# A decoder layer in split float32 on one core: the ten seven-product pairs of the last product at every second place instead of partly two in a row

## The chip, the core and the metric

The kernel runs on one core of a Trainium2 chip. The core has a matrix engine (TensorE, PE in the profile; its weight loads are listed apart as PEld), a vector engine (DVE), a scalar engine (ACT), a GpSimd engine (POOL) and a queue that issues transfers (SP). The engines run their own instruction lists in order and wait for each other through semaphores; transfers between main memory and the on-chip memory run beside them. The metric is the time of one execution on the device in microseconds (us).

## What is computed

One decoder layer for 256 tokens of width 2048, in float32. A first half (attention, a gated matrix memory, gates, an output projection) is left as it is by the change. The second half is a gated feed-forward block with a short convolution:

```python
h2 = rmsnorm(x, norm2_g[l])
u = causal_dwconv(jnp.einsum('bsd,df->bsf', h2, w_up[l]), conv_w[l], conv_b[l])
u_gate, u_val = u[..., :D_FF], u[..., D_FF:]
x = x + jnp.einsum('bsf,fd->bsd', jax.nn.silu(u_gate) * u_val, w_down[l])
```

`D_FF` is 5632. The last line holds the last product, which the change is about: 256 x 5632 by 5632 x 2048, added to x.

## The kernel before

**Split operands.** Every float32 operand is split in two: a high part that the matrix engine's fast float32 form takes exactly (`wh` for a weight), and the rest (`wl`). A product is three matmuls: high weight with both parts of the activation, low weight with its high part. Splitting weights is work for two engines. For each piece of a weight chunk ACT copies it into `wh` (line 169) and DVE subtracts to get `wl` (line 170). `wh` and `wl` have three buffers each, so piece n can only be split when PE has finished piece n - 3.

**Chunks and pairs.** Weights arrive in chunks of 1 MB (`raw`, three buffers, SP queue, line 132). In the last product one chunk is a pair: two steps of 128 along the 5632, by 1024 columns. There are 22 pairs for each of two column blocks, called y0 and y1 after their tiles. The accumulators of a block are `y0q` and `y0p` (or `y1q`, `y1p`).

**Two kinds of pair.** A plain pair ("p") is two pieces of 1024 columns and eight products of 128 x 512, 24 matmuls. A seven-product pair ("S") does the same block by a Strassen-like scheme with seven products, 21 matmuls. It has four pieces: "b" (1024 columns, straight from `raw`), "b21" (512 columns, straight from `raw`), "t13" (1024, sums) and "t24" (1024, sums). The sums of weights are formed by DVE in one tile `sums`: line 154 (1024 columns, the t13 half), line 161 and line 164 (512 each, the t24 half). The sums of activations were formed once in the stage before and stored in main memory (`se`, `s_dram`, lines 934 to 940); line 952 brings them back on POOL's queue, one load of 768 KB (`s_ops`) for two S pairs. Three such tiles fit at first; the next load waits until the tile of two S pairs ago has been read for the last time, and in y1 the tiles of finished activations come free as well. After the last S pair of a block the four sums of products are added into the result (line 298) while the remaining plain pairs run, then the plain accumulators (line 974), and the result goes out.

**What sets the order.** `Y_PAIRS` (line 39) gives the kind of each of the 22 pairs, for both blocks. `next_sub(3)` (line 175) splits three pieces ahead. A scheduler then orders each engine's list and may move an instruction ahead of others: it puts line 154 for the next S pair, which needs only the next chunk, early, between the two sums pieces of the S pair now in work. All lines 154 stand behind the last step of the up stage on DVE (the split of the last activations, `ghl`, line 196; the order is asked for in line 153). The stage before (up) computes `ghl`; its last matmuls, evacuation and split overlap the first pair of y0.

Chunks are numbered through the program: `raw204` is pair 0 of y0, `raw226` pair 0 of y1; pieces are numbered too, `wl434` being the first of y0.

Of the kernel before, what the change touches and what calls it, by code (L numbers as in the profile page):

```python
# [35 lines left out]
PLAIN = "p" * 8  # L36
G_PAIRS = "pSpSpSpp"
WO_PAIRS = "pSpSpppp"
Y_PAIRS = "ppp" + "SSpSp" * 3 + "Sp" + "pp"
N_S = Y_PAIRS.count("S")  # L40


# [18 lines left out]
def trunk(ctx: ExitStack, tc: tile.TileContext, a):  # L61
# [44 lines left out]
    def add_pairs(ap, patterns):  # L106
        for i, kind in enumerate("".join(patterns)):
            pieces = ("b", "b21", "t13", "t24") if kind == "S" else ("whole", "whole")
            add_chunk(ap[i], 2048, pieces)
# [8 lines left out]
    subs_of[n + 1], subs_of[n + 2] = subs_of[n + 2], subs_of[n + 1]  # L118
    add_pairs(a["w_dn"], [Y_PAIRS] * 2)

# [800 lines left out]
    for j in range(NF):  # L921
# [11 lines left out]
        m = j // 2  # L933
        if Y_PAIRS[m] == "S":
            se = big.tile([P, 2, 3 * P], F32R, tag="mv", name=f"se{m}")
# [7 lines left out]

    s_pos = [m for m, kind in enumerate(Y_PAIRS) if kind == "S"]
    ring = []
# [8 lines left out]
    def sums_of(b, m):  # L954
        g, (r, i) = g_pairs[m], divmod(s_pos.index(m) + b * N_S, 2)
        if i == 0:
            load_sums()
        at = [ring[r][:, q * P : (q + 1) * P] for q in range(6 * i, 6 * i + 6)]
        return [(g[:, 0, 0, P:], g[:, 0, 1, P:])] + [(at[c], at[3 + c]) for c in range(3)]
# [3 lines left out]
    for b in range(2):  # L963
# [5 lines left out]
        y_ops = Lazy(lambda m, b=b: sums_of(b, m))  # L969
        q = s_block(f"y{b}", g_pairs, y_ops, Y_PAIRS, pools, dst)  # L970
        for h in range(2):
# [80 lines left out]
```

## Time and profile before

| what | us |
|---|---|
| median of three runs (lowest, highest) | 1402.92 (1402.15, 1404.12) |
| the profiled execution's own time | 1393.67 |
| its span | 1391.9 |
| block y0, first matmul to first of y1 | 1150.7 to 1269.7 |
| block y1, first matmul to last | 1269.7 to 1387.2 |

The profiled execution is some 9 us shorter than the median of the runs shown, and differences are taken against its own time. The page's first part gives busy time by engine over the whole span: PE 99 %, DVE 77 %, ACT 55 %. A busy PE includes matmuls whose modelled ends overlap the next start, so small stalls must be read from starts in the timeline, where rows give start, duration, engine, line, operation, tiles and count, and in brackets the idle time before and what ended it.

### The profile page before, as it was taken

How to read it: one execution, taken by the hardware profiler on the slowest of the kernel's cores; microseconds unless marked ns; L12 is line 12 of the kernel's file. 1: busy time of each engine (PE TensorE's matmuls, PEld its weight loads, DVE VectorE, ACT ScalarE, POOL GpSimd, SP SyncE). 2: the span in 40 equal slices, each digit the busy share in tenths (PEclk: the TensorE clock that was granted, in tenths of full speed). 3: DMA queues.
4: the chain of work that ended last, by engine and by line, in shares of the span. 5: the costliest groups of instructions: out<-in, count | busy, mean ns of one | idle time of the engine just before them, and what ended most of it. 6: DMA issues, size and time to landing. Idle time of an engine off the chain costs nothing.

```text
span 1391.9 us, 18433 instructions
## 1 busy us (share of the span) xinstructions
PE 1375.6 (99%) x6940; PEld 1157.2 (83%) x6940; DVE 1070.9 (77%) x1524; ACT 767.2 (55%) x1096; POOL 40.4 (3%) x73
## 2 busy tenths in 40 slices
PE   9999999999999999999999999999999999999998
PEld 8878888887888888888888888888888887778776
DVE  5655766556888867777878888888878888887987
ACT  6645554444665544555655555555655655553553
POOL 2101000000000000000000000000000000000000
PEclk9999999999999999999999999999999999999999
DMA  8645454443554565555555655655555657668553
GB/s 312 229 165 184 179 209 155 152 151 134 196 215 182 214 241 194 190 220 203 191 186 194 218 193 190 222 186 196 201 212 194 230 196 266 226 251 291 205 209 119
DMA packets 44073, 281.76 MB, mean 202 GB/s; under 512 B 5008, under 2 KB 5024, under 8 KB 13264
## 3 DMA queue, kind: packets, MB, share of 16 engines
q1 hardware_dynamic: 39168, 260.20, 52.4%
q0 software_dynamic: 4672, 20.38, 4.2%
q8 instruction: 54, 0.88, 0.2%
q14 instruction: 35, 0.29, 0.1%
q10 hardware_dynamic: 144, 0.02, 0.0%
HBM read 272.45 MB, written 8.13 MB: 202 GB/s over the span
## 4 chain that ended last, share of the span: by engine, by line
PE 96%; DVE 1%; issue 1%; ACT 1%; DMA 1%; POOL 0%; DVEq 0%; ACTq 0%; POOLq 0%
PE up L230 35%; PE p L230 6%; PE y1q L230 6%; PE y0q L230 5%; PE mog L230 3%; PE fq L230 3%; PE mv L230 3%; PE fk L230 3%; PE fv L230 3%; PE wo0q L230 3%; PE wo1q L230 3%; PE g1q L230 2%; PE g3q L230 2%; PE g2q L230 2%; PE g0q L230 2%; PE y1p L230 2%
## 5 line engine op out<-in xcount | busy, mean ns | idle before, releaser
L169 ACT ACTIVATE wh<-raw 128x1024 fp32r<-128x1024 f32 (+2 forms) x496 | 502.7, 1017 | 473.9 <-PE up L230 117.9
L170 DVE TENSOR_TENSOR wl<-raw,wh 128x1024 fp32r<-128x1024 f32 (+2 forms) x496 | 575.1, 1169 | 205.3 <-ACT wh L169 203.5
L230 PE MATMUL up<-h,wh 128*128 128x512 f32 x1408 | 488.6, 394 | 0.0
L230 PE MATMUL up<-h,wl 128*128 128x256 f32 x1408 | 390.0, 277 | 0.0
L230 PEld LDWEIGHTS up<-h,wh 128*128 128x128 f32 x1408 | 263.9, 188 | 61.4 <-DVE h L199 0.2
L230 PEld LDWEIGHTS up<-h,wl 128*128 128x128 f32 x1408 | 264.4, 188 | 0.1
L170 DVE TENSOR_TENSOR wl<-sums,wh 128x1024 fp32r<-128x1024 f32 x66 | 80.6, 1222 | 43.9 <-ACT wh L169 43.5
L169 ACT ACTIVATE wh<-sums 128x1024 fp32r<-128x1024 f32 x66 | 69.9, 1060 | 78.6 <-PE y0q L230 16.6
L909 DVE SCALAR_TENSOR_TENSOR t<-u,cst,t 128x256 f32<-128x256 f32 x176 | 84.7, 481 | 3.8 <-ACT t L907 0.7
L230 PE MATMUL p<-wh,am 128*128 128x512 f32 x256 | 79.6, 392 | 0.0
L230 PE MATMUL y1q<-wh,ghl 128*128 128x512 f32 x232 | 71.7, 390 | 0.0
L230 PE MATMUL y0q<-wh,ghl 128*128 128x512 f32 x232 | 71.7, 390 | 0.0
L230 PEld LDWEIGHTS p<-wh,am 128*128 128x128 f32 x256 | 47.6, 188 | 9.7
L907 ACT ACTIVATE t<-u,cst 128x256 f32<-128x256 f32 x88 | 52.0, 591 | 2.4 <-DVE u L904 1.9
L230 PEld LDWEIGHTS y1q<-wh,ghl 128*128 128x128 f32 x232 | 43.6, 188 | 9.2
L230 PEld LDWEIGHTS y0q<-wh,ghl 128*128 128x128 f32 x232 | 43.5, 188 | 9.1
L230 PE MATMUL p<-wl,am 128*128 128x512 f32 x128 | 49.9, 390 | 0.0
L230 PE MATMUL y1q<-wl,ghl 128*128 128x512 f32 x116 | 44.8, 391 | 0.0
L230 PE MATMUL y0q<-wl,ghl 128*128 128x512 f32 x116 | 44.8, 390 | 0.0
L154 DVE TENSOR_TENSOR sums<-raw 128x1024 f32<-128x1024 f32 x33 | 40.4, 1223 | 4.7 <-DMA raw<-in_w_dn 3.0
L230 PE MATMUL mog<-wh,hT 128*128 128x348 f32 (+1 forms) x192 | 42.4, 331 | 1.3 <-ACT wh L169 1.3
L230 PE MATMUL g0q<-wh,hN 128*128 128x512 f32 x128 | 41.3, 401 | 0.0
(370 smaller groups left out, 2064.0 us busy)
## 6 DMA issues: line engine op xcount, KB each, us to landing
raw<-in_w_up SPq DMA_DIRECT2D x88, 1024.0 KB, 4.9
raw<-in_w_dn SPq DMA_DIRECT2D x44, 1024.0 KB, 4.9
raw<-in_w_g SPq DMA_DIRECT2D x32, 1024.0 KB, 4.9
raw<-in_w_fox SPq DMA_DIRECT2D x24, 1024.0 KB, 4.9
raw<-in_w_p SPq DMA_DIRECT2D x16, 1024.0 KB, 4.8
raw<-in_w_out SPq DMA_DIRECT2D x16, 1024.0 KB, 4.8
raw<-in_w_mqk SPq DMA_DIRECT2D x8, 1024.0 KB, 4.8
raw<-in_w_mv SPq DMA_DIRECT2D x8, 1024.0 KB, 4.8
```

Source lines behind the costliest of these rows:

```text
L154: nc.vector.tensor_tensor(sums[:, :1024].rearrange("p (i c) -> p i c", i=2), raw[:, :512].unsqueeze(1).to_broadcast([P, 2, 512]), src.rear ...
L169: nc.scalar.activation(wh[:, :n], src, AF.Copy)
L170: nc.vector.tensor_tensor(wl[:, :n], src, wh[:, :n].bitcast(F32), ALU.subtract)
L230: nc.tensor.matmul(out, lhsT, rhs, start=start, stop=stop)
L907: nc.scalar.activation(t, u[:, 2:], AF.Identity, scale=w[2], bias=w[3])
L909: nc.vector.scalar_tensor_tensor(out=t, in0=u[:, i : i + S], scalar=w[i], in1=t, op0=ALU.mult, op1=ALU.add)
```

## The change

One line. `Y_PAIRS` was `pppSSpSpSSpSpSSpSpSppp` (S pairs at places 3, 4, 6, 8, 9, 11, 13, 14, 16 and 18) and becomes `pSpSpSpSpSpSpSpSpSpSpp` (places 1, 3, 5 and so on to 19). There are ten S and twelve p in both, so the number of matmuls, splits, sums and bytes is the same.

```diff
-Y_PAIRS = "ppp" + "SSpSp" * 3 + "Sp" + "pp"
+Y_PAIRS = "p" + "Sp" * 10 + "p"
```

The scheduler's order changes with it. At the end of the up stage, DVE's list before, from the last activations (`gv`, `ghl`) to the first sums; the first S pair is `raw207`, and `raw206` is still a plain pair:

```order
L170 TENSOR_TENSOR wl437_10360<-raw205_10274,wh437_10359 128x1024
L909 SCALAR_TENSOR_TENSOR t_10320<-u0_5502,cst_75,t_10320 128x256 x2
L930 TENSOR_TENSOR gv_10218<-sg_10271,t_10320 128x256
L170 TENSOR_TENSOR wl438_10378<-raw206_10337,wh438_10377 128x1024
L196 TENSOR_TENSOR ghl10_5500<-gv_10218,ghl10_5500 128x2x256
L154 TENSOR_TENSOR sums207_10411<-raw207_10375 128x1024
L170 TENSOR_TENSOR wl439_10394<-raw206_10337,wh439_10393 128x1024
L161 TENSOR_TENSOR sums207_10411<-raw207_10375,sums207_10411 128x512
```

The same place of the changed kernel's list, where the first S pair is `raw205` and `wl437` is its piece b21:

```order
L170 TENSOR_TENSOR wl437_10363<-raw205_10274,wh437_10362 128x512
L909 SCALAR_TENSOR_TENSOR t_10320<-u0_5502,cst_75,t_10320 128x256 x2
L930 TENSOR_TENSOR gv_10218<-sg_10271,t_10320 128x256
L196 TENSOR_TENSOR ghl10_5500<-gv_10218,ghl10_5500 128x2x256
L154 TENSOR_TENSOR sums205_10343<-raw205_10274 128x1024
L161 TENSOR_TENSOR sums205_10343<-raw205_10274,sums205_10343 128x512
L164 TENSOR_TENSOR sums205_10343<-raw205_10274,sums205_10343 128x512
L170 TENSOR_TENSOR wl438_10384<-sums205_10343,wh438_10383 128x1024
L170 TENSOR_TENSOR wl439_10398<-sums205_10343,wh439_10397 128x1024
```

The first sums still stand behind the last activations, but now they belong to the second pair of y0, not to the fourth; `wl438` and `wl439` are its pieces t13 and t24.

Further on, DVE's list before where two S pairs follow each other (`raw207`, `raw208`), from the split of the first one's t13 to that of the second one's t24:

```order
L170 TENSOR_TENSOR wl442_10452<-sums207_10411,wh442_10451 128x1024
L154 TENSOR_TENSOR sums207_10411<-raw208_10409 128x1024
L170 TENSOR_TENSOR wl443_10466<-sums207_10411,wh443_10465 128x1024
L170 TENSOR_TENSOR wl444_10474<-raw208_10409,wh444_10473 128x1024
L161 TENSOR_TENSOR sums207_10411<-raw208_10409,sums207_10411 128x512
L170 TENSOR_TENSOR wl445_10485<-raw208_10409,wh445_10484 128x512
L164 TENSOR_TENSOR sums207_10411<-raw208_10409,sums207_10411 128x512
L170 TENSOR_TENSOR wl446_10498<-sums207_10411,wh446_10497 128x1024
L170 TENSOR_TENSOR wl447_10508<-sums207_10411,wh447_10507 128x1024
```

The changed kernel's list over one period, from the S pair `raw209` over the plain pair `raw210` to the S pair `raw211`:

```order
L170 TENSOR_TENSOR wl450_10542<-sums205_10343,wh450_10541 128x1024
L154 TENSOR_TENSOR sums205_10343<-raw211_10538 128x1024
L170 TENSOR_TENSOR wl451_10552<-sums205_10343,wh451_10551 128x1024
L170 TENSOR_TENSOR wl452_10559<-raw210_10500,wh452_10558 128x1024
L170 TENSOR_TENSOR wl453_10569<-raw210_10500,wh453_10568 128x1024
L170 TENSOR_TENSOR wl454_10582<-raw211_10538,wh454_10581 128x1024
L161 TENSOR_TENSOR sums205_10343<-raw211_10538,sums205_10343 128x512
L170 TENSOR_TENSOR wl455_10599<-raw211_10538,wh455_10598 128x512
L164 TENSOR_TENSOR sums205_10343<-raw211_10538,sums205_10343 128x512
L170 TENSOR_TENSOR wl456_10618<-sums205_10343,wh456_10617 128x1024
```

Two plain pieces (`wl452`, `wl453`) now always stand between the pieces of two S pairs, and line 154 for the next S pair always stands ahead of the split of the current one's t24 (`wl451`). Before, that was so at the same relation of pairs only where a p stood between.

## The prediction

> **What bounds the kernel now.** I first read the busy time of the two blocks of the last product (windows view: us, then busy us of PE, PEld, DVE, ACT, POOL, then granted clock, DMA share, GB/s).
>
> ```profile
> 1150.70:1269.70 119.00, 115.14 (x500) 91.76 (x499) 101.80 (x112) 63.46 (x69) 3.19 (x6) 1.00 0.68 246
> 1269.70:1387.20 117.50, 115.08 (x499) 91.54 (x498) 99.38 (x105) 60.38 (x64) 1.79 (x3) 1.00 0.56 202
> ```
>
> PE is the busiest engine, at full clock, with DVE not far behind. What PE needs at its own pace comes from two rows of the timeline, three matmuls apart, in a plain pair:
>
> ```profile
> 1155.51 0.62 PE L230 MATMUL y0q<-wh,ghl 128*128 128x512 f32 x2
> 1156.19 0.62 PE L230 MATMUL y0q<-wh,ghl 128*128 128x512 f32 x2
> ```
>
> One product takes 0.68 us. A block has 12 x 8 + 10 x 7 = 166 products, so 112.9 us. y0 loses 119.0 - 112.9 = 6.1 us, y1 117.5 - 112.9 = 4.6 us: all that a better order can win in the two blocks is 10.7 us. Where it is lost, by the waits view from 1140 to the end (who waited for whom: total us, times, longest):
>
> ```profile
> DVE sums L154 <- DMA raw<-in_w_dn: 3.0, 2, 1.7
> PEld y0p L230 <- DVE wl L170: 3.7, 10, 1.9
> PEld y1p L230 <- ACT wh L169: 3.7, 3, 1.2
> PEld y0p L230 <- ACT wh L169: 3.7, 3, 1.2
> PEld y1p L230 <- DVE wl L170: 2.1, 10, 0.3
> ```
>
> Three waits for `wh` in each block are the three places with two S pairs in a row. One wait for `wl` in y0 is 1.9 us long, and the others are small; and line 154 waited for a chunk twice, 1.7 us the longer. In the up stage this view lists no wait of PE of any size, so where the activation sums are formed there does not matter.
>
> **What the change removes.** At a double place DVE falls behind, because the second S pair follows with four pieces and 2048 columns of sums before a plain pair gives air. PE rows at the first such place:
>
> ```profile
> 1174.48 0.63 PE L230 MATMUL y0p<-wh,s_ops 128*128 128x512 f32 x2
> 1175.92 0.51 PE L230 MATMUL y0p<-wh,s_ops 128*128 128x512 f32 x1 [0.81 <-ACT wh L169]
> 1176.26 0.40 PE L230 MATMUL y0p<-wl,ghl 128*128 128x512 f32 x1
> ```
>
> Two matmuls from 1174.48 end their turn at 1174.93; the next starts 0.99 late, and the one after it 0.11: 1.1 us. An S pair between plain pairs loses hardly anything:
>
> ```profile
> 1188.15 0.45 PE L230 MATMUL y0p<-wl,s_ops 128*128 128x512 f32 x1
> 1188.44 0.40 PE L230 MATMUL y0q<-wl,ghl 128*128 128x512 f32 x1
> ```
>
> That is 0.06 late; with another small gap I count 0.1. So six double places give back 6 x (1.1 - 0.1) = 6.0 us.
>
> The 1.9 us wait has another cause. PE, DVE, and the chain that ended last (start, length):
>
> ```profile
> 1240.44 1.07 PE L230 MATMUL y0q<-wh,ghl 128*128 128x512 f32 x4
> 1242.96 0.50 PE L230 MATMUL y0p<-wl,s_ops 128*128 128x512 f32 x1 [1.46 <-DVE wl L170]
> 1243.30 0.40 PE L230 MATMUL y0q<-wl,ghl 128*128 128x512 f32 x1
> ...
> 1237.67 1.23 DVE L170 TENSOR_TENSOR wl<-sums,wh 128x1024 fp32r<-128x1024 f32 x1 [0.97 <-ACT wh L169]
> 1240.55 1.23 DVE L154 TENSOR_TENSOR sums<-raw 128x1024 f32<-128x1024 f32 x1 [1.66 <-DMA raw<-in_w_dn]
> ...
> 1232.65 7.81 DMA raw<-in_w_dn
> ```
>
> Line 154 for the next S pair stands ahead of the split of the current t24. Its chunk, issued at 1232.65, landed 7.8 us later, and DVE waited 1.66 us with that split queued behind; PE came 1.61 + 0.11 = 1.7 us late. So **a late chunk goes through to PE in full**. This place gives 1.6 us more than a quiet single S. It disappears as it stands, and I count 7.6 us removed in all.
>
> **What the change adds: the first S pair of y0.** It is now pair 1. DVE and ACT at the end of the up stage:
>
> ```profile
> 1156.77 0.43 DVE L930 TENSOR_TENSOR gv<-sg,t 128x256 f32<-128x256 f32 x1
> 1157.30 1.23 DVE L170 TENSOR_TENSOR wl<-raw,wh 128x1024 fp32r<-128x1024 f32 x1
> 1158.44 0.68 DVE L196 TENSOR_TENSOR ghl<-gv,ghl 128x512 fp32r<-128x512 f32 x1
> ...
> 1157.22 0.63 ACT L195 ACTIVATE ghl<-gv 128x512 fp32r<-128x512 f32 x1
> 1158.94 1.06 ACT L169 ACTIVATE wh<-raw 128x1024 fp32r<-128x1024 f32 x1 [1.08 <-PE y0q L230]
> ```
>
> By the new order a half-width split (0.68 us, as the half-width row above, instead of 1.23) stands ahead of `gv`, and the split between `gv` and `ghl` is gone. So `gv` starts at about 1156.2, ACT's part of `ghl` runs 1156.7 to 1157.3, DVE's to 1158.0, then line 154 (1.23) to 1159.2 and ACT's `wh` of t13 (1.06) to 1160.3. PE starts y0 at 1150.7, so it wants t13 after 8 + 3 products, at 1158.2. It waits 2.1 us, once. In y1 there is no `ghl`, and the chunk of pair 1 is loaded long before: nothing.
>
> **What it adds in every period.** In steady state S and p take 15 products and 0.1, that is 10.3 us. The rows of an S pair that follows a p:
>
> ```profile
> 1184.43 1.23 DVE L170 TENSOR_TENSOR wl<-sums,wh 128x1024 fp32r<-128x1024 f32 x1 [0.96 <-ACT wh L169]
> 1185.69 1.22 DVE L154 TENSOR_TENSOR sums<-raw 128x1024 f32<-128x1024 f32 x1
> ...
> 1190.34 0.33 SPq L132 DMA_DIRECT2D raw<-in_w_dn  x1
> ```
>
> After line 154 come t24's split and the two of the plain pair; then that pair's buffer is free and SP issues the load, 4.65 us after line 154 began. In the new order this load is the chunk of the S pair after next, and line 154 wants it one period later: it has 10.3 - 4.65 = **5.65 us to land**. At the place above it had 6.24 (1237.67 and the 1.22 of that split, against 1232.65), because the double place had stretched the period. A quiet chunk lands in 4.9 (first row below, the median of all). But chunks issued 1.3 to 2.2 us behind a load of `s_ops` are later. POOL's rows, then the six chunks issued at 1179.4, 1201.4, 1216.9, 1232.7, 1254.9 and 1293.8 (KB, us to landing):
>
> ```profile
> raw<-in_w_dn SPq DMA_DIRECT2D x44, 1024.0 KB, 4.9
> ...
> 1178.11 0.53 POOL L952 DMA_DIRECT2D s_ops<-s_dram  x1 [26.40 <-PE y0q L230]
> 1231.33 0.53 POOL L952 DMA_DIRECT2D s_ops<-s_dram  x1 [15.29 <-PE y0q L230]
> 1281.09 0.56 POOL L952 DMA_DIRECT2D s_ops<-s_dram  x1 [6.30 <-PE y1q L230]
> 1291.85 0.53 POOL L952 DMA_DIRECT2D s_ops<-s_dram  x1 [10.20 <-PE y1q L230]
> ...
> raw<-in_w_dn SPq DMA_DIRECT2D x1, 1024.0 KB, 5.6
> raw<-in_w_dn SPq DMA_DIRECT2D x1, 1024.0 KB, 6.9
> raw<-in_w_dn SPq DMA_DIRECT2D x1, 1024.0 KB, 7.3
> raw<-in_w_dn SPq DMA_DIRECT2D x1, 1024.0 KB, 7.8
> raw<-in_w_dn SPq DMA_DIRECT2D x1, 1024.0 KB, 6.6
> raw<-in_w_dn SPq DMA_DIRECT2D x1, 1024.0 KB, 7.0
> ```
>
> Mean 6.87, from 5.6 to 7.8. Before, only the 7.8 met an early line 154 that it could make wait; the other late ones were for chunks wanted later, or landed in time. In the new order the load of `s_ops` comes at the end of every second S pair, some 2 us ahead of just the chunk with 5.65 us to land. It does so after the second, fourth, sixth and eighth S pair of y0 and, as the last two rows allow, after pairs 1 and 3 of y1: six places. Each costs PE the landing less 5.65: between 0 (5.6) and 2.15 (7.8), and by the mean 1.22. I take the mean, as five of the six rows lie near it: 6 x 1.22 = 7.3 us, bounds 0 and 12.9.
>
> The end moves little: after the last S pair two plain pairs remain instead of three, 10.9 us, and DVE's eight sums and four splits (0.68 and 1.23 each, so 10.4) fit; if they don't, the last line 974 is late by under 1 us.
>
> **Sum.** -7.6 + 2.1 + 7.3 = +1.8 us: 1393.67 becomes 1395.5, and the median of the runs 1402.92 becomes 1404.7. About 0.2 % (2.8 us) is what a measurement can tell from no change here, so the likeliest outcome is within it.
>
> **Rivals.** (1) *The six chunks land early enough.* If two transfers share the engines without loss and the first has its lead, all land like the 5.6: no wait is left, -7.6 + 2.1 = -5.5, 1397.4. Halfway to the mean, at 6.2, it is -2.2, 1400.7. For it speaks one row of six, against it the five others. The Trainium skill, "DMA: Bandwidth & Descriptors", section on the anatomy of one DMA on the SWDGE path, gives a transfer about 2.0 us fixed and its bytes at 436 GB/s. By that rule, as an estimate, the 768 KB ahead add at most 1.8 us to the 4.4 of a chunk, 6.2, and the change would come out slightly faster. The trace has 6.6 to 7.8 in five of six, so the rule has little behind it here.
> (2) *Slower.* The six places are all like the one that the chain shows, 7.8: 12.9 us of waits, -5.5 + 12.9 = +7.4, 1410.3. The sign turns where the mean landing passes 6.57 (5.65 and 5.5 over 6); it is measurably slower from 7.03 and measurably faster below 6.1. For it speaks that a second chunk follows 3 us behind in each period, as at the 7.3; against it the mean of the rows.
> (3) *It doesn't remove what it says.* DVE's lag comes from every S pair, and single ones wait too: the 6.0 stay, +7.8, 1410.7. Against it stand the row pair with 0.06 and the fact that DVE's work for S and p together (six steps of 1.23 and three of 0.68, 9.4 us) fits in 10.3.
>
> **How the numbers follow.** The forecast has 0.66, with its own range 1402 to 1407.5 (mean landing 6.4 to 7.3); rival 1 has 0.17, rival 2 0.12, rival 3 0.05. Faster by over 0.2 %: 0.13 of rival 1 and 0.01 of the forecast, 0.14. Slower: 0.19 of the forecast (landing above 7.03) and rivals 2 and 3, 0.36. Within: 0.50. The range 1399 to 1409 leaves out the best half of rival 1 and most of rivals 2 and 3.
>
> **What would show it.** Right: no wait of PE for ACT's `wh` at t24 in the middle of a block; one of about 2 us at the first t13 of y0, near 1158; some five or six waits of line 154 for `raw`, 0.5 to 2 us each, at every second S pair in y0 and twice early in y1, and PE as late each time; none later in y1, where no `s_ops` is left to load. Wrong: line 154 waits less than 3 us in all (rival 1) or over 11 (rival 2), or `wh` waits at single S pairs (rival 3).

## The result: 0.8 % slower

The changed kernel takes 1414.54 us (median of six runs, 1412.01 to 1419.44) against 1403.92 (six runs, 1402.15 to 1406.87). The ratio is 1.0084, 95 % interval [1.0061, 1.0106], so the change costs some 11 us: 10.6 by the medians, 8.6 to 14.9 by the interval.

The up stage of either kernel takes 489 us in some executions and 498 in others, so y0 begins near 1151 or near 1160; why stays open. Below, the two blocks are therefore compared, from the first matmul of y0 to the last of y1, and not whole times. The profiled execution of the changed kernel, 1419.44 us with a span of 1417.6, began y0 at 1160.1, that of before at 1150.7.

The two blocks by the windows view of the changed kernel (us, busy us of PE, PEld, DVE, ACT, POOL, granted clock, DMA share, GB/s), y0 and y1:

```profile
1160.10:1292.50 132.40, 121.84 (x500) 96.50 (x499) 101.84 (x112) 64.05 (x69) 3.18 (x6) 0.95 0.62 218
1292.50:1412.70 120.20, 114.69 (x498) 91.68 (x498) 98.89 (x106) 61.05 (x64) 1.79 (x3) 1.00 0.56 200
```

y0 grew from 119.0 to 132.4 us and y1 from 117.5 to 120.2: 252.6 against 236.5, 16.1 us more. The clock of y0 is 0.95, where before it was 1.00. The waits view of the changed kernel, from 1140 to the end (total us, times, longest):

```profile
DVE sums L154 <- DMA raw<-in_w_dn: 15.8, 7, 2.8
...
PEld y0p L230 <- DVE wl L170: 11.6, 10, 2.7
...
PEld y1p L230 <- DVE wl L170: 8.5, 11, 3.0
...
PEld y0p L230 <- ACT wh L169: 2.7, 2, 2.3
```

The waits for ACT's `wh` at double places (3.7 us in each block before) are gone, but for those at one place at the start of y0. In their place line 154 waits 15.8 us for chunks (3.0 before), and PE waits for `wl` behind it. One such place, the second of y0. The rows of the timeline are POOL's load, SP's issue of the chunk, DVE's list and PE's, and the last row, from the table of issues, is that chunk (KB, us to landing):

```profile
1209.98 0.53 POOL L952 DMA_DIRECT2D s_ops<-s_dram  x1 [24.12 <-PE y0q L230]
...
1211.43 0.33 SPq L132 DMA_DIRECT2D raw<-in_w_dn  x1
...
1219.41 1.22 DVE L154 TENSOR_TENSOR sums<-raw 128x1024 f32<-128x1024 f32 x1 [2.32 <-DMA raw<-in_w_dn]
1220.55 1.22 DVE L170 TENSOR_TENSOR wl<-sums,wh 128x1024 fp32r<-128x1024 f32 x1
...
1218.68 1.07 PE L230 MATMUL y0q<-wh,ghl 128*128 128x512 f32 x4
1221.83 0.74 PE L230 MATMUL y0p<-wl,s_ops 128*128 128x512 f32 x1 [2.08 <-DVE wl L170]
1222.36 0.63 PE L230 MATMUL y0q<-wl,ghl 128*128 128x512 f32 x1
1222.79 1.48 PE L230 MATMUL y0q<-wh,ghl 128*128 128x512 f32 x3
...
raw<-in_w_dn SPq DMA_DIRECT2D x1, 1024.0 KB, 7.5
```

The chunk was issued at 1211.43, 1.45 us behind the load of `s_ops`, and landed after 7.5 us. DVE waits 2.32 with t24's split (line 170) behind line 154, and PE's first matmul on that `wl` starts 2.24 late (four matmuls of 0.227 from 1218.68 end their turn at 1219.59). That is the forecast's chain. What the forecast did not have stands in the last two rows of PE: the next matmuls start 0.43 us apart and not 0.23. The windows view around that stall (the granted clock is the last column but two):

```profile
1219.50:1221.80 2.30, 0.25 (x2) 0.00 (x0) 2.30 (x3) 0.00 (x0) 0.00 (x0) 1.00 0.18 71
1221.90:1223.60 1.70, 1.70 (x4) 1.36 (x5) 1.70 (x2) 1.01 (x1) 0.00 (x0) 0.50 0.00 0
1223.60:1225.30 1.70, 1.70 (x5) 1.32 (x4) 1.70 (x3) 0.00 (x0) 0.00 (x0) 0.50 0.32 43
1225.40:1227.40 2.00, 2.00 (x10) 1.64 (x9) 0.87 (x2) 0.63 (x1) 0.00 (x0) 1.00 0.84 340
```

For 3.4 us TensorE ran at half clock: nine matmuls in 3.4 us, where at full clock ten take 2.0 to 2.3. That loses another 1.7 us. PE counts as busy there, so neither the busy share nor the waits view shows it.

All places of the changed kernel's profile, from starts in the timeline (PE late; the landing of the chunk that line 154 waited for):

| place | PE late, us | chunk landed after, us | half clock behind it |
|---|---|---|---|
| 1169.65, first t13 of y0 | 2.03 | no chunk: behind `ghl` | yes |
| 1197.25 | 2.35 | 8.0, behind `s_ops` | yes |
| 1221.83 | 2.24 | 7.5, behind `s_ops` | yes |
| 1246.47 | 2.35 | 8.0, behind `s_ops` | no |
| 1269.58 | 2.39 | 8.0, behind `s_ops` | yes |
| 1305.08 (y1) | 2.30 | 8.4, beside the stores of y0's result | no |
| 1318.18 (y1) | 2.72 | 8.4, behind `xr` (the input that y1 is added to) and `s_ops` | no |
| 1329.51 (y1) | 0.95 | 6.6, behind `s_ops` | no |

The seven late chunks make 15.3 us, and four stretches at half clock 4 x 1.7 = 6.8.

### The profile page after: what moved, and what is told of

Its sections match the earlier page's. It is cut to its first block, busy times and chain, and to the rows that moved or that the text cites. A ratio compares the mean times of both kernels' runs of the same rounds, so it can differ in the third digit from the quotient of the medians.

```text
span 1417.6 us, 18438 instructions
## 1 busy us (share of the span) xinstructions
PE 1391.3 (98%) x6940; PEld 1166.3 (82%) x6940; DVE 1071.7 (76%) x1524; ACT 766.4 (54%) x1096; POOL 40.4 (3%) x73
## 4 chain that ended last, share of the span: by engine, by line
PE 90%; DMA 4%; DVE 3%; issue 2%; ACT 1%; POOL 0%; DVEq 0%; ACTq 0%; POOLq 0%
PE up L230 35%; PE p L230 6%; PE y1q L230 5%; DMA raw<-in_w_dn 3%; PE y0q L230 3%; PE mog L230 3%; PE fq L230 3%; PE mv L230 3%; PE fk L230 3%; PE fv L230 3%; PE wo0q L230 3%; PE wo1q L230 3%; DVE wl L170 2%; PE g2q L230 2%; PE g3q L230 2%; PE g1q L230 2%
## 5 line engine op out<-in xcount | busy, mean ns | idle before, releaser
L170 DVE TENSOR_TENSOR wl<-raw,wh 128x1024 fp32r<-128x1024 f32 (+2 forms) x496 | 574.2, 1170 | 211.9 <-ACT wh L169 209.7
L230 PE MATMUL up<-h,wh 128*128 128x512 f32 x1408 | 497.8, 399 | 0.0
L230 PE MATMUL up<-h,wl 128*128 128x256 f32 x1408 | 395.2, 281 | 0.0
L230 PEld LDWEIGHTS up<-h,wh 128*128 128x128 f32 x1408 | 264.5, 188 | 66.3 <-DVE h L199 0.2
L230 PEld LDWEIGHTS up<-h,wl 128*128 128x128 f32 x1408 | 266.0, 189 | 0.1
L170 DVE TENSOR_TENSOR wl<-sums,wh 128x1024 fp32r<-128x1024 f32 x66 | 80.7, 1223 | 53.0 <-ACT wh L169 53.0
L230 PE MATMUL p<-wh,am 128*128 128x512 f32 x256 | 79.6, 392 | 0.0
L230 PE MATMUL y0q<-wh,ghl 128*128 128x512 f32 x232 | 73.8, 405 | 0.0
L230 PE MATMUL y1q<-wh,ghl 128*128 128x512 f32 x232 | 70.3, 390 | 0.0
L230 PEld LDWEIGHTS p<-wh,am 128*128 128x128 f32 x256 | 47.6, 188 | 9.7
L230 PEld LDWEIGHTS y0q<-wh,ghl 128*128 128x128 f32 x232 | 45.6, 197 | 10.2
L154 DVE TENSOR_TENSOR sums<-raw 128x1024 f32<-128x1024 f32 x33 | 40.4, 1225 | 17.4 <-DMA raw<-in_w_dn 15.8
L230 PEld LDWEIGHTS y1q<-wh,ghl 128*128 128x128 f32 x232 | 43.6, 188 | 9.2
L230 PE MATMUL p<-wl,am 128*128 128x512 f32 x128 | 49.9, 390 | 0.0
L230 PE MATMUL y0q<-wl,ghl 128*128 128x512 f32 x116 | 46.1, 410 | 0.0
L230 PE MATMUL y1q<-wl,ghl 128*128 128x512 f32 x116 | 43.9, 391 | 0.0
L230 PE MATMUL mog<-wh,hT 128*128 128x348 f32 (+1 forms) x192 | 42.3, 330 | 1.4 <-ACT wh L169 1.4
L230 PE MATMUL g0q<-wh,hN 128*128 128x512 f32 x128 | 41.3, 401 | 0.0
```

Source lines behind the costliest of these rows:

```text
L154: nc.vector.tensor_tensor(sums[:, :1024].rearrange("p (i c) -> p i c", i=2), raw[:, :512].unsqueeze(1).to_broadcast([P, 2, 512]), src.rear ...
L170: nc.vector.tensor_tensor(wl[:, :n], src, wh[:, :n].bitcast(F32), ALU.subtract)
L230: nc.tensor.matmul(out, lhsT, rhs, start=start, stop=stop)
```

## The experiments

Nine further runs follow; two of them are the two kernels as they are. Those with a ratio ran eight to ten times, the others once. In some of them edits shift line numbers by a few: L157, L173 and L235 there are L154, L170 and L230 of the changed kernel.

### Both kernels again

> The kernel before, unchanged, profiled a second time, to see what belongs to the execution and not to the change. In the first profiles the up stage took 488.8 us before and 498 us with the change, with PE never waiting in either. If that is a property of the execution, this profile may show an up stage near 498 us as well; if the change slows the up stage (theory U: the activation sums at other pairs), it is 488.8 us again. Block y0 119.0 us and y1 117.5 us in either case, with one late chunk at most.

> The changed kernel, unchanged, profiled a second time. Theory L (late chunks): the same six or seven waits of line 154 for a chunk, each 2.3 to 2.8 us, and line 154 some 16 us in all. Theory C (clock): after some of these waits PE runs at half its granted clock for about 2 us; which ones is not fixed, so the number of slow stretches may differ from the four of the first profile. Theory U: the up stage takes 498 us here and 488.8 us in the kernel before.

The kernel before took 1403.3 us, the changed one 1404.22 in a single execution. Their blocks start at 1160.3 and 1152.3, so these two whole times hide the difference. Here the kernel before has the late start and the changed one the early start, the other way round from the first profiles, so the start belongs to the execution and not to the change. The blocks took 236.5 and 245.4 us, 8.9 apart. The changed kernel's blocks:

```profile
1152.30:1276.60 124.30, 115.54 (x500) 91.88 (x499) 101.56 (x112) 63.98 (x69) 3.19 (x6) 1.00 0.65 233
1276.60:1397.70 121.10, 116.39 (x499) 92.78 (x497) 98.96 (x106) 60.99 (x64) 1.79 (x3) 0.99 0.56 198
```

The gaps at the four places of y0 are 1.85, 2.08, 1.52 and 2.04, in y1 1.70 at the stores and 2.88 behind `xr` and `s_ops`; the last reload of y1 costs nothing this time, but a chunk with no other load near it (6.2 us) costs 0.61 at 1355.56. Together 12.7 us; the first t13 waits 2.05. Line 154 waited 13.2 us for chunks, where some 16 were expected. But y0 kept its full clock, and only the 2.88 was followed by a slow stretch; that one began 0.4 us before PE resumed and cost 1.5 us. So the waits come with the order of the program, and the slow clock with some executions of it.

### Line 154 behind the plain pair's splits

In line 153, for every S pair of y0 and y1 but the first:

```diff
-            with tc.issue_after(last_of["up"].ins) if "up" in last_of else nullcontext():
+            behind = last_of.get("wl") if "sums" in last_of else last_of.get("up")
+            if "up" in last_of:
+                last_of["sums"] = True
+            with tc.issue_after(behind.ins) if behind is not None else nullcontext():
...
+        last_of["wl"] = nc.vector.tensor_tensor(
```

> The changed kernel with line 154 queued on DVE behind the last split made before it, so that it stands behind the next plain pair's two splits and no longer ahead of the current t24's split. A chunk then has some 3.4 us more to land, 9 us instead of 5.65. Theory L: the late chunks (8.0 us) are hidden, the six places cost nothing, the slow clock goes with them, and only the one wait of 2.1 us at the first S pair of y0 is left: 5 to 6 us faster than before, ratio 0.996. If the cost lies in the up stage (theory U) or in the first S pair, it stays 8 us or more slower than before.

The order of pairs is the changed one, and line 154 now comes after t24's split and the two splits of the plain pair. DVE's list there, over the same stretch as the late place of 1197.25 above:

```profile
1190.95 2.59 DVE L173 TENSOR_TENSOR wl<-sums,wh 128x1024 fp32r<-128x1024 f32 x2 [1.38 <-ACT wh L172]
1193.46 2.35 DVE L173 TENSOR_TENSOR wl<-raw,wh 128x1024 fp32r<-128x1024 f32 x2
1195.73 1.22 DVE L157 TENSOR_TENSOR sums<-raw 128x1024 f32<-128x1024 f32 x1
```

Line 154 (L157 here) starts at 1195.73 with no idle time before it. Its chunk, issued at 1185.53, landed after 7.5 us, at 1193.0: **the chunk is as late as before, and nobody waits for it**. The blocks:

```profile
1159.95:1277.43 117.48, 115.61 (x501) 93.21 (x499) 101.63 (x112) 64.07 (x69) 3.19 (x6) 0.99 0.70 246
1277.43:1391.20 113.77, 113.77 (x499) 92.00 (x497) 98.86 (x106) 60.95 (x64) 1.79 (x3) 1.00 0.59 211
```

231.2 us, 5.3 less than before the change; ratio 0.9947 [0.9916, 0.9978]. The only stall left is the first t13 of y0, 2.03 us, with half clock behind it; y1 has none.

### The chunks without the reloads

```diff
-        if len(ring) < N_S:
+        if 3 <= len(ring) < N_S:
+            ring.append(ring[-3])
+        if len(ring) < 3:
```

This leaves out seven of the ten loads of `s_ops`; the later S pairs use sums of other pairs.

> The changed kernel without the last seven of the ten loads of the activation sums: the three tiles of the first three loads are used over and over, so the seven-product pairs from the seventh on use sums of other pairs. Line 154 stays where it was. Theory L: without these loads the chunks land in about 4.9 us, inside the 5.65, line 154 waits for next to nothing, and the time is 5 to 6 us under before (ratio 0.996), like the kernel with line 154 moved. If chunks are late for another reason (two chunks 3 us apart), the waits stay.

Chunks issued from 1188 to 1265, in the table of issues (KB, median us to landing):

```profile
raw<-in_w_dn SPq DMA_DIRECT2D x16, 1024.0 KB, 4.8
```

All sixteen landed within 4.7 to 5.0 us, and in y0 no late chunk is left. The late places of y0 are thus the reload's doing. In y1 one place stays: the chunk issued at 1271.63, between the stores of y0's result, took 8.2 us and PE came 2.14 late, with no `s_ops` in flight. That is the place that the forecast had not listed. A chunk with nothing near it (6.3 us) cost another 0.64 at 1345.32. The blocks took 235.5 us, and the ratio is 1.0005 [0.9971, 1.0039], not the 0.996 expected. With the reload's waits gone, the first t13 (2.04, and 1.7 at half clock behind it) and the two places in y1 still cost 6.5 us. Without them the blocks would have taken 229.0, so the new order by itself gives 7.5 us, and these places take back most of it.

### Line 154 late, and the first one early too

As in the experiment with line 154 behind the plain pair's splits, and line 153 now sets the first sums of y0 behind the last split as well, so that they no longer wait for the last `ghl`:

```diff
-            behind = last_of.get("wl") if "sums" in last_of else last_of.get("up")
-            if "up" in last_of:
-                last_of["sums"] = True
+            behind = last_of.get("wl") if "up" in last_of else None
```

> As e1_late_sums (line 154 of every S pair behind the splits of the plain pair), and now also the first one of y0, which in e1 still waited for the end of the up stage. Theory (the clock belongs to the stall): the 2.0 us wait at the first t13 of y0 goes, and with it the matmuls at half clock behind it, about 1.7 us more: y0 and y1 together 231.2 - 2.1 - 1.7 = 227.4 us, ratio to the kernel before about 0.992. Rival (the half clock comes from the change of stage, not from the stall): only the 2.1 goes, 229.1 us, and slow matmuls still show near 1170.

```profile
1160.59:1274.47 113.88, 113.88 (x501) 92.09 (x499) 100.90 (x112) 64.20 (x69) 3.17 (x6) 1.00 0.72 254
1274.47:1388.20 113.73, 113.73 (x499) 91.99 (x497) 98.87 (x106) 60.95 (x64) 1.79 (x3) 1.00 0.60 211
```

PE is busy for the whole of both windows, at full clock: 227.6 us, within 0.2 of the expected 227.4, and 1.8 above the 225.8 that 332 products need. No slow stretch shows near 1170, so the rival that put it down to the change of stage falls. The ratio to the kernel before is 0.9953 [0.9928, 0.9978] (medians 1394.89 and 1403.55). The 0.992 expected misses that interval; it did not follow from its own sum either, as 9 us of 1403 make 0.9936. **This version beats both kernels.** Against the one with the first sums late its blocks are 3.6 us shorter in the profiles; the two ratios do not tell them apart.

### The old order of pairs with line 154 late

The same edit as in the first experiment on line 153, in the kernel before.

> The old order of the pairs with line 154 behind the splits of the plain pair, as in e1. If e1 gains because it has no double places and no late chunks both, this gains only the one late-chunk place: y0 and y1 together 236.4 - 1.6 = 234.8 us, the six gaps of 1.0 at the double places stay, ratio about 0.999. Rival: line 154's early place was what cost time at the double places too; then most of the six gaps go as well and the blocks take about 229 to 231 us, ratio about 0.995.

The waits view of this kernel from 1140 to the end:

```profile
PEld y0p L235 <- ACT wh L172: 3.7, 3, 1.2
PEld y1p L235 <- ACT wh L172: 3.7, 3, 1.2
...
PEld y0p L235 <- DVE wl L173: 2.2, 10, 0.3
```

The six waits at double places are where they were, and the long wait for `wl` is gone. The blocks took 235.3 us, 1.2 less than before (expected 1.6); ratio 0.9983 [0.9956, 1.0009]. The interval holds 1, so this gain is not clear of noise. Neither edit alone does it: the late line 154 takes out late chunks, the new order takes out double places, and together, with the first sums early as well, they give 8.9 us in the blocks.

### The reload on SP's queue

```diff
-            nc.gpsimd.dma_start(ring[-1], s_dram[:, i : i + 12 * P])
+            nc.sync.dma_start(
+                ring[-1].bitcast(F32), s_dram[:, i : i + 12 * P].bitcast(F32)
+            )
```

> The changed kernel with the loads of s_ops issued on SP's queue, which also carries the chunks, instead of POOL's. Bytes theory: two chunks and a load of 768 KB share the same engines whichever queue they are on, so the chunk behind the load still lands after 7.5 to 8.0 us and line 154 still waits 2 us or more at six places; y0 and y1 together 245 to 253 us. Queue theory: the load on POOL's queue is slower to serve than one on SP's and holds the chunk up; then the chunk lands after 6.2 to 6.6, the waits are 0.6 to 1.0 each, no half clock, and the blocks take about 238 us.

Issues from 1206.2 to 1208.2, a reload and the chunk 1.71 us behind it:

```profile
raw<-in_w_dn SPq DMA_DIRECT2D x1, 1024.0 KB, 6.0
s_ops<-s_dram SPq DMA_DIRECT2D x1, 768.0 KB, 4.1
```

Behind the reloads of y0 the chunks landed after 6.4, 6.0, 6.1 and, once, 7.9 us, where the changed kernel had 7.5 to 8.0, and the blocks took 241.2 us against 252.6 and 245.4, between the two ranges expected (some 238, and 245 to 253). The waits of PE in y0 were 0.78, 0.74, 0.48 and 2.33, and a fifth of 0.93 at a chunk (6.5) with no reload near it; half clock followed the 2.33. Three of four places are as the queue theory has it, one is not, and the chunk stood 1.71 us behind the load here and 1.45 in the changed kernel, so its distance may have a part in it. This is one execution, and a lead rather than a proof.

### The reload in halves

First, each load of 768 KB as two of 384 KB into the two halves of the same tile, the second asked for one S pair later:

```diff
+        c = slice(0, 12 * P) if half is None else slice(half * 6 * P, (half + 1) * 6 * P)
+        nc.gpsimd.dma_start(ring[-1][:, c], s_dram[:, i + c.start : i + c.stop])
```

> The changed kernel with each load of 768 KB brought in two halves of 384 KB, one behind each S pair, so every chunk with 5.65 us to land has 384 KB ahead of it instead of every second one 768 KB. Bytes theory: the landing grows with the bytes, 4.9 + (8.0 - 4.9) / 2 = 6.4 us, so some 13 waits of 0.8 to 0.9 us, 11 us in all, and no matmuls at half clock behind them, since gaps of 1.6 us or less never showed that; y0 and y1 together about 232 + 2 + 11 = 245 us. Rival (a load costs the same whatever its size): 8.0 us at each place, 13 waits of over 2 us and half clock behind many, 265 us or more.

This was no test of either theory. Both halves wait for the same tile to come free, and POOL issued them together:

```profile
1185.11 1.06 POOL L957 DMA_DIRECT2D s_ops<-s_dram  x2 [22.22 <-PE y0q L230]
```

The chunks behind them in y0 landed after 7.5, 7.4, 6.8 and 8.5 us, the blocks took 248.2: as with one load. So it was made again with a tile of its own for each S pair:

```diff
-            ring.append(a8(f"s_ops{len(ring)}", [12 * P], F32R))
-            nc.gpsimd.dma_start(ring[-1], s_dram[:, i : i + 12 * P])
+            ring.append(a8(f"s_ops{len(ring)}", [6 * P], F32R))
+            nc.gpsimd.dma_start(ring[-1], s_dram[:, i : i + 6 * P])
```

> The changed kernel with one tile of s_ops for each seven-product pair (384 KB) instead of one for two (768 KB), three tiles as before, so each tile comes free at another time and a load of 384 KB stands ahead of the chunk of every period. In e8_half_reloads the two halves were issued together behind one release and changed nothing; here they cannot be. Bytes theory: 4.9 us without a load, 7.4 to 8.0 with 768 KB, so 6.2 to 6.5 with 384 KB; against 5.65 that is 13 or more waits of 0.5 to 0.9 us, none long enough for half clock except the 2.0 at the first t13; y0 and y1 together 238 to 243 us. Rival (each load on POOL's queue costs the chunk behind it a fixed 2.5 to 3 us): landings of 7.4 to 8.0 every period, twice as many waits of 2 us, half clock behind some, 260 us or more.

POOL's rows for a reload in y0 and one in y1, and the blocks:

```profile
1219.56 0.53 POOL L952 DMA_DIRECT2D s_ops<-s_dram  x1 [10.85 <-PE y0q L230]
...
1311.27 1.06 POOL L952 DMA_DIRECT2D s_ops<-s_dram  x2 [12.01 <-PE y1q L230]
```

```profile
1160.05:1284.93 124.88, 116.51 (x500) 91.88 (x499) 101.54 (x112) 63.95 (x69) 5.81 (x11) 1.00 0.67 224
1284.93:1410.80 125.87, 116.87 (x499) 92.79 (x497) 98.96 (x106) 60.94 (x64) 4.42 (x8) 0.99 0.58 200
```

In y0 one load of 384 KB stands ahead of each chunk, and from 1184 to 1264 eight places lose 0.59 to 1.33 us, none followed by half clock; their chunks landed after 6.3 to 7.2 us. With none it is 4.7 to 5.0 and with 768 KB 7.1 to 8.0, so in y0 the landing grows with the bytes ahead. But the sum expected for both blocks (238 to 243) missed: it was 250.7. In y1 two tiles come free at a time, two loads go out together (x2), the chunks behind them take 7.5 to 8.3 us again, and three places lose 1.84 to 2.71 each, the last of them with half clock behind it, besides 2.21 at the stores. Both kernels with smaller loads ran once.

## Why the prediction was wrong

**What held, in place and in size.** The six double places gave their waits back: no wait for `wh` is left there. The new order gives 7.5 us by the kernel without the reloads, once its four remaining losses are taken off; the forecast counted 7.6. (The 8.9 us of the best version also hold 1.4 us of gaps under 0.35 us: these sum to 3.1 us before and to 1.7 there.) The first t13 of y0 waited 2.03 us with 2.1 forecast. The budget of 5.65 us holds: in the second profile of the changed kernel the four landings of y0 average 7.4, which less 5.65 is 1.75, and PE came 1.87 late on average. All six places of the forecast had their wait in the first profile and five in the second, and PE was late by about as much as line 154 each time.

**The step that failed: the size of the six landings.** "I take the mean, as five of the six rows lie near it: 6 x 1.22 = 7.3 us." The row of 5.6 was the odd one. A chunk issued 1.3 to 1.5 us behind the reload, as the new order has it each time, landed in y0 after 5.6, 7.3, 7.8 and 6.6 in the profile of before; the same chunks took 6.3, 7.4, 7.6 and 7.2 in its second profile, 7.7, 7.3, 7.3 and 7.3 in the old order with line 154 late. Chunks 1.9 us or more behind the reload took 6.9 and 7.0 in the first profile, but 5.0 to 5.9 in these two. The mean of 6.87 thus put two kinds together. That did not move it, as the first kind alone has 6.8 in that profile; what did was one execution, since the same chunks average 7.1 and 7.4 in the other two. In the changed kernel y0's four were 8.0, 7.5, 8.0, 8.0 and, the second time, 7.5, 7.3, 7.1, 7.7. The six places cost 13.0 and 10.4 us in its two profiles, where 7.3 was forecast: near rival 2's 12.9, which had a chance of 0.12. Line 154 waited 15.8 and 13.2 us, past the 11 that the prediction names as rival 2's sign. From the Trainium skill, "DMA: Bandwidth & Descriptors", section on the anatomy of one DMA on the SWDGE path, the prediction had estimated 6.2 us for such a chunk. No chunk behind a reload on POOL's queue landed so early in y0 of the changed kernel, and three of four behind one on SP's came within 0.2 of it.

**A place left out.** The chunk issued between the third and the fourth store of y0's result landed after 8.4 us and cost 2.30 (1.70 the second time, at 7.8 us). Before, no early line 154 met it. In two of the eight profiles of the new order the chunk at that place landed after 6.0 us, and what made the difference was not shown. The forecast went through the loads of `s_ops` and did not look for other transfers near a chunk with 5.65 us to land. For the same reason the first of its two places in y1 was dearer than any in y0: `xr` lay ahead as well.

**A term left out: the clock.** Every stall was priced at its own length. In the first profile four stalls cost 1.7 us more each at half clock: 6.8 us for a term that the forecast put at nothing, more than the 5.6 by which its six places were too cheap. The sum goes through with it (us, from the forecast's +1.8 for the blocks):

| | first profile | second profile |
|---|---|---|
| four places of y0 (forecast 4.9) | 9.3: +4.4 | 7.5: +2.6 |
| two reload places of y1 (forecast 2.4) | 3.7: +1.2 | 2.9: +0.4 |
| the place at the stores | +2.3 | +1.7 |
| a chunk late by itself | 0 | +0.6 |
| half clock | +6.8 | +1.5 |
| sum with the +1.8 | +16.5 | +8.6 |
| measured in the blocks | +16.1 | +8.9 |

The median of the runs, 10.6 us above the median of before, lies between the two.

**Rivals.** Rival 1 (chunks early enough) falls with the landings. Rival 3 (single S pairs wait as the double ones do) falls with the two kernels that have line 154 late in the new order: no single S pair waits there. Rival 2 named the right cause, with its size nearly right, but had neither the stores nor the clock.

What stays open: why y0's landings were 0.5 us longer in the first profile of the changed kernel than in the second, and which part of a landing is the queue's and which the bytes'. No experiment took the two apart over more than one execution.

## What to carry to other kernels

An instruction that waits for a transfer should not stand in an in-order list ahead of work whose inputs are ready. Here three splits moved ahead of line 154 hid the late landings (7.2 to 7.6 us in y0), which had cost 10 to 13 us in both blocks, and the reordering of pairs that had looked bad became the better order. When a transfer's slack is to be compared with landings, group the rows by what else is in flight and how far ahead, take several executions, and go through every other transfer of the stage, stores included. And price a stall of 2 us or more on a saturated TensorE with the slow clock that may follow it.

## What was not expected of the hardware

**Half clock after stalls of about 2 us, by the phase of a fixed period.** Every slow stretch lasted 3.4 us. In the first profile of the changed kernel they began at 1170.71, 1198.03, 1221.91 and 1269.70: 27.32, 51.20 and 98.99 us from the first, which are 8, 15 and 29 times 3.414. The two slow stretches of the kernel with loads in halves lie 58.03 apart, 17 times 3.413. So the clock looks at fixed periods of 3.41 us. Laying each profile's stalls of 0.9 us or more on such a grid, set by its own first slow stretch, gives 39 stalls in seven profiles, of which 11 were followed by half clock. Each of these 11 had 2.03 us or more within one period. Of the other 28 one, at 1318.18 in the first profile, had as much to within 0.02, and the next has 1.88. So the border lies near 2.03 us and no sharper than that. The stall at 1246.47, 2.35 long, straddled a border as 1.68 and 0.67 and was not followed by one:

```profile
1244.20:1246.40 2.20, 0.08 (x1) 0.00 (x0) 2.20 (x3) 0.00 (x0) 0.00 (x0) 1.00 0.12 52
1246.50:1248.20 1.70, 1.70 (x8) 1.34 (x9) 1.70 (x2) 1.06 (x1) 0.00 (x0) 1.00 0.00 0
```

The clock stays at 1.00 with eight matmuls in 1.7 us, against four at 1221.90 above. That the idle time within one period decides fits all of these, but for that one at the border, and no kernel was made to test it alone. The Trainium skill, "TensorE: Matmul & The Clock Gate", section "What's actually happening", states a free-running window of 3413 ns, and the traces agree with it; its section on HAM oscillation puts the rule as no gaps over some 3.4 us, and here a gap of 2.03 us was enough.
